# A hybrid decoder layer: k's normed blocks in the convolution's buffers, k's products in the common banks, v's first products bank by bank, and the square root behind the exponentials

## The chip, the cores and the metric

The program runs on one core of a Trainium2 chip. The metric is the device time of one execution in microseconds (us). Five engines work side by side, each through its own queue in the order written there: TensorE (PE, matrix products), VectorE (DVE), ScalarE (ACT), GpSimd (POOL) and SyncE (SP, which only issues transfers). An instruction that waits holds back everything behind it on its engine.

## The reference, cut to what matters

```python
x = x + 0.5 * swiglu(rms_norm(x, g1), ...)          # first feed-forward
h = rms_norm(x, gm)
xr, gate, q, k, v = split(h @ w_in)                 # 512 columns each
xc = causal_conv4(xr) + conv_b                      # RG-LRU branch
r, i = sigmoid(blockdiag(w_a) xc + b_a), sigmoid(blockdiag(w_x) xc + b_x)
a = exp(8 * r * log_sigmoid(lam));  b = sqrt(1 - a * a) * (i * xc)
h_t = a_t * h_(t-1) + b_t                           # a scan over 512 positions
y_rnn = h * gelu(gate)
q, k = rms_norm per head of 64;  z = q @ k.T        # stick-breaking attention
w = exp(log_sigmoid(z) + sum of log_sigmoid(-z) over the later keys);  y_att = w @ v
x = x + concat(rms_norm(y_rnn), rms_norm(y_att)) @ w_out
x = x + 0.5 * swiglu(rms_norm(x, g2), ...)          # second feed-forward
```

All data is float32; the sequence has 512 positions and the model 1024 columns.

## The kernel before, in words

Every large product is three matrix products of rounded parts (`mm3`, lines 137 to 139): weights and activations are split into a high part `h_`/`xh_` (a copy on ACT, line 127) and a low part `l_`/`xl_` (a subtraction on DVE, line 129). Weights come in by SP through three raw buffers `r_` and four buffers each of `h_` and `l_`.

The layer has a first feed-forward (`a`), the mixer, and a second feed-forward (`b`). The change lies in the mixer's projections, about 435 to 500 us into the span. There TensorE runs the column blocks one after another: four pairs of recurrence input and gate (`pxr`, `pga`, j = 0 to 3), then q after the second pair, k after the last, then v. Each of q, k and v is a set of four accumulators, one per 128 positions (`pk0` to `pk3`, `pv0` to `pv3`), filled over four weight tiles (`h_v0` to `h_v3`), each of two rows of 128 model columns. So a weight tile stands for 24 matrix products. Accumulators live in eight banks of PSUM, six under the tag `b` and two under the tag `y`, which are handed out in turn.

`gate(j)` computes the two block-diagonal products `pa`, `px` of the convolved block (in `xch`/`xcl`) in the two `y` banks. ACT makes of them `dec` (sigmoid), `tau` (tanh) and `ix` (sigmoid), and POOL multiplies `ix` by the convolved block. After the last, `gate(3)`, `recur` runs: exponentials of `dec`, one square root over all of `tau` (2048 columns), and on DVE, for each j, `ix` times `tau`, a second multiplication with `dec`, and the scan into `tau`. POOL multiplies the scan into `gel`. `rnn_out` splits `gel` into `yrh` (ACT) and `yrl` (DVE), and its squares are added up on POOL in `sqa_r`.

`norm_heads` norms k per head: ACT squares the accumulator (`nsqk`), DVE sums per head (`m8k`), POOL takes the power -0.5 (`r8k`), and DVE writes the normed block (`natk`) from the accumulator, which sets that bank free. `turn` transposes `natk` on TensorE into `ptk` (in a `y` bank); ACT and DVE write the split result `kTh`, `kTl`. When v's products are done, the sum of squares `pst_r`, the first output projection `po` and the attention's scores `pz` follow.

The order on each engine is not the order of the source: a scheduler orders the instructions at build time by its own estimate of times, and `issue_after` ties an instruction behind another. SP's order is the same in both kernels.

Of the kernel before, what the change touches and what calls it, by code (L numbers as in the profile page):

```python
# [8 lines left out]
F32 = mybir.dt.float32  # L9
F32R = mybir.dt.float32r  # L10
BF16 = mybir.dt.bfloat16
AF = mybir.ActivationFunctionType
# [3 lines left out]
P = 128  # L16
T = 512
D = 1024
KD = D // P
DFF = 2816  # L20
NF = DFF // P
DR = 512
NJ = DR // P
NB = T // P
# [25 lines left out]
def hybrid_layer_kernel(  # L50
# [17 lines left out]
    nc = tc.nc  # L68
# [21 lines left out]
    def bank(name, tag="b"):  # L90
        return banks["pool"].tile([P, T], F32, tag=tag, name=name, bufs=banks["tags"][tag])
# [40 lines left out]
    def weights_early(*args):  # L132
        with tc.high_priority(offset=200):
            return weights(*args)

    def mm3(out_, wh, wl, ah, al, start, stop):
        nc.tensor.matmul(out_, wh, ah, start=start, stop=False)  # L137
        nc.tensor.matmul(out_, wh, al, start=False, stop=False)  # L138
        nc.tensor.matmul(out_, wl, ah, start=False, stop=stop)  # L139
# [338 lines left out]
    neg_c = mp.tile([P, NJ], F32, tag="neg_c", name="neg_c", bufs=1)  # L478
# [19 lines left out]
    rp = rnn.enter_context(tc.tile_pool(name="rnn", bufs=1, reuse_waits="tile"))  # L498
    tau = rp.tile([P, NJ, T], F32, tag="tau", name="tau")
    dec = rp.tile([P, NJ, T], F32, tag="dec", name="dec")  # L500
# [66 lines left out]
    def recur():  # L567

        with tc.issue_after(box["gate"].ins):
            for j in range(NJ):  # L570
                nc.scalar.activation(dec[:, j, :], dec[:, j, :], AF.Exp, scale=neg_c[:, j : j + 1])
        last = nc.scalar.activation(tau, tau, AF.Sqrt)
        with tc.issue_after(last.ins):
            nc.scalar.activation(warm, mhalf, AF.Sigmoid)
        for j in range(NJ):
            nc.vector.tensor_mul(ix[j], ix[j], tau[:, j, :])
            nc.vector.scalar_tensor_tensor(
                ix[j], dec[:, j, :], 1.0, ix[j], op0=ALU.add, op1=ALU.mult
            )
            nc.vector.tensor_tensor_scan(  # L580
                tau[:, j, :], dec[:, j, :], ix[j], 0.0, op0=ALU.mult, op1=ALU.add
            )
            nc.gpsimd.tensor_mul(gel[j], gel[j], tau[:, j, :])
# [18 lines left out]
    v = []  # L602

    def project_qkv(c, n, between):
        pts = [bank(f"p{n}{b}", "y" if n == "k" and b < 2 else "b") for b in range(NB)]
        done = 0
        for kk in range(KD // 2):
            wh, wl = weights_early(w_qkv[c, kk], f"{n}{kk}")
            ks = (2 * kk, 2 * kk + 1)
            order = [(k, b) for k in ks for b in range(NB)]  # L610
            if kk == KD // 2 - 1:
                order = [(k, b) for b in range(NB) for k in ks]
            for k, b in order:
                t = slice(b * P, (b + 1) * P)
                s = slice((k % 2) * DR, (k % 2 + 1) * DR)
                mm3(pts[b], nm.h[k][:, t], nm.l[k][:, t], wh[:, s], wl[:, s], k == 0, k == KD - 1)
                done += 1
                if done in between:
                    between[done]()
        return pts  # L620

    def heads(ap):
        return ap.rearrange("p (h d) -> p h d", h=NH)

    def norm_heads(n, pts):
        nats = []
        for b in range(NB):
            rb = nm.r[:, b : b + 1]
            sq = rp.tile([P, DR], F32, tag="nsq", name=f"nsq{n}{b}", bufs=1)
            nc.scalar.activation(sq, pts[b], AF.Square, scale=rb)  # L630
            m = stat.tile([P, NH], F32, tag="m8", name=f"m8{n}{b}")
            nc.vector.tensor_reduce(m, heads(sq), axis=mybir.AxisListType.X, op=ALU.add)
            nc.vector.tensor_scalar(m, m, 1.0 / HD, EPS, op0=ALU.mult, op1=ALU.add)
            r = stat.tile([P, NH], F32, tag="r8", name=f"r8{n}{b}")
            nc.gpsimd.tensor_tensor(r, m, mhalf, op=ALU.pow)
            nat = rp.tile([P, DR], F32, tag="nat", name=f"nat{n}{b}", bufs=3)
            nc.vector.scalar_tensor_tensor(
                heads(nat),
                heads(pts[b]),
                rb,  # L640
                r.unsqueeze(2).to_broadcast([P, NH, HD]),
                op0=ALU.mult,
                op1=ALU.mult,
            )
            nats.append(nat)
        return nats
# [21 lines left out]
    convolve(0, *pj[0])  # L668
    convolve(1, *pj[1])
    pq = project_qkv(0, "q", {16: lambda: gate(0), 28: lambda: gate(1)})  # L670
    nq = norm_heads("q", pq)
    pj.append(project(2))
    convolve(2, *pj[2])
# [4 lines left out]
    def gate_and_recur():  # L678
        gate(3)
        recur()  # L680

    pk = project_qkv(1, "k", {8: gate_and_recur})
    nk = norm_heads("k", pk)
    pv = project_qkv(2, "v", {12: rnn_out, 27: lambda: turn("k", nk)})
    for b in range(NB):
        rb = nm.r[:, b : b + 1]
# [267 lines left out]
```

## Time and profile before

| what | value |
|---|---|
| median of 3 runs | 952.56 us (951.93 to 954.64) |
| the profiled execution | 952.85 us |
| its span, first to last instruction | 951.1 us |
| mean granted TensorE clock | 0.991 |
| busy PE | 928.4 us, 98% of the span |
| busy DVE | 675.0 us, 71% |
| busy ACT | 375.2 us, 39% |
| busy POOL | 111.1 us, 12% |

TensorE is busy nearly throughout, so a change can shorten the run only where TensorE stands idle or runs at a lower clock. In the rows, a time of one instruction is from its start to its end; matrix products overlap, so the pace of a row of them is read from the distance of their starts.

### The profile page before, as it was taken

What the parts mean: (1) busy time and instruction counts of PE and PEld (TensorE: products, weight loads), DVE (VectorE), ACT (ScalarE), POOL (GpSimd) and SP (SyncE); (2) the same over time, 40 slices, a digit from 0 to 9 for tenths busy, and PEclk for the clock granted to TensorE, in tenths of its full rate; (3) what the DMA queues carried; (4) which work ended last, traced back from release to release, by engine and by line L of the source; (5) the groups of instructions that cost most, each with busy time, mean ns of one, the idle gap of its engine ahead of it and who ended that gap; (6) DMA issues with size and microseconds to landing.
All of it is one profiled execution on the core that took longest, in us unless ns stands there. A gap on an engine that the chain in (4) does not pass through costs nothing.

```text
span 951.1 us, 12503 instructions
## 1 busy us (share of the span) xinstructions
PE 928.4 (98%) x4906; PEld 787.1 (83%) x4906; DVE 675.0 (71%) x1001; ACT 375.2 (39%) x529; POOL 111.1 (12%) x79
## 2 busy tenths in 40 slices
PE   8999999999999999999958999999999999999998
PEld 6888988898889888888845667888998899889987
DVE  7687867786768559673588867477776777677753
ACT  7233333333334334452647743343343333333430
POOL 4000000000000005543351121500000000000000
PEclk9999999999999999999979999999999999999999
DMA  7530443044302423322111112421152125212312
GB/s 244 178 110 1 151 138 111 1 135 154 110 2 72 150 75 116 120 84 83 34 34 34 45 67 89 159 100 52 67 178 89 66 68 177 89 67 67 105 52 89
DMA packets 27066, 89.44 MB, mean 94 GB/s; under 512 B 3072, under 2 KB 5376, under 8 KB 27008
## 3 DMA queue, kind: packets, MB, share of 16 engines
q1 hardware_dynamic: 27008, 88.65, 27.4%
q8 instruction: 39, 0.64, 0.3%
q14 instruction: 19, 0.16, 0.1%
HBM read 86.54 MB, written 2.10 MB: 93 GB/s over the span
## 4 chain that ended last, share of the span: by engine, by line
PE 87%; DVE 6%; DMA 3%; issue 1%; ACT 1%; SPq 1%; POOL 0%; DVEq 0%; ACTq 0%
PE pda L343 9%; PE pdb L343 8%; PE pga L137 5%; PE pga L139 5%; PE pga L138 5%; PE pub L137 4%; PE pub L139 4%; PE pgb L137 4%; PE pub L138 4%; PE pgb L139 4%; PE pgb L138 4%; PE pua L137 4%; PE pua L139 4%; PE pua L138 4%; PE po L137 1%
## 5 line engine op out<-in xcount | busy, mean ns | idle before, releaser
L343 PE MATMUL pdb<-bhb,l_db 128*128 128x256 f32 x252 | 70.6, 284 | 0.7 <-DVE l_db L129 0.7
L343 PE MATMUL pda<-bha,h_da 128*128 128x256 f32 x252 | 71.2, 284 | 0.0
L343 PE MATMUL pdb<-bhb,h_db 128*128 128x256 f32 x252 | 71.2, 284 | 0.0
L343 PE MATMUL pda<-bla,h_da 128*128 128x256 f32 x252 | 71.0, 283 | 0.0
L343 PE MATMUL pdb<-blb,h_db 128*128 128x256 f32 x252 | 71.0, 283 | 0.0
L343 PE MATMUL pda<-bha,l_da 128*128 128x256 f32 x252 | 70.5, 284 | 0.2 <-DVE l_da L129 0.2
L137 PE MATMUL pub<-xh_b,h_ub 128*128 128x512 f32 x176 | 68.7, 390 | 0.5 <-DVE yo L702 0.5
L137 PE MATMUL pgb<-xh_b,h_gb 128*128 128x512 f32 x176 | 68.6, 390 | 0.0
L139 PE MATMUL pgb<-xh_b,l_gb 128*128 128x512 f32 x176 | 68.5, 389 | 0.0
L138 PE MATMUL pgb<-xl_b,h_gb 128*128 128x512 f32 x176 | 68.5, 389 | 0.0
L138 PE MATMUL pub<-xl_b,h_ub 128*128 128x512 f32 x176 | 68.5, 389 | 0.0
L139 PE MATMUL pub<-xh_b,l_ub 128*128 128x512 f32 x176 | 68.5, 389 | 0.0
L137 PE MATMUL pga<-xh_a,h_ga 128*128 128x512 f32 x160 | 62.4, 390 | 0.0
L137 PE MATMUL pua<-xh_a,h_ua 128*128 128x512 f32 x160 | 62.3, 390 | 0.0
L139 PE MATMUL pga<-xh_a,l_ga 128*128 128x512 f32 x160 | 62.3, 389 | 0.0
L138 PE MATMUL pga<-xl_a,h_ga 128*128 128x512 f32 x160 | 62.3, 389 | 0.0
L139 PE MATMUL pua<-xh_a,l_ua 128*128 128x512 f32 x160 | 62.3, 389 | 0.0
L138 PE MATMUL pua<-xl_a,h_ua 128*128 128x512 f32 x160 | 62.2, 389 | 0.0
L167 POOL TENSOR_TENSOR sqa_m<-sqa_m,sq_m 128x512 f32<-128x512 f32 x7 | 11.8, 1680 | 325.9 <-issue 322.1
L343 PEld LDWEIGHTS pdb<-bhb,l_db 128*128 128x128 f32 x252 | 47.8, 192 | 1.2 <-DVE l_db L129 1.1
L246 DVE TENSOR_TENSOR uub<-pub,rb_b 128x512 f32<-128x512 f32 x22 | 15.2, 690 | 47.4 <-PE pub L139 47.4
L343 PEld LDWEIGHTS pda<-bha,h_da 128*128 128x128 f32 x252 | 48.3, 192 | 0.5
(318 smaller groups left out, 2460.4 us busy)
## 6 DMA issues: line engine op xcount, KB each, us to landing
r_gb<-in_wg SPq DMA_DIRECT2D x22, 512.0 KB, 3.3
r_ub<-in_wu SPq DMA_DIRECT2D x22, 512.0 KB, 3.3
r_ga<-in_wg SPq DMA_DIRECT2D x20, 512.0 KB, 3.3
r_ua<-in_wu SPq DMA_DIRECT2D x20, 512.0 KB, 3.4
rda<-in_wd SPq DMA_DIRECT2D x12, 768.0 KB, 4.9
rdb<-in_wd SPq DMA_DIRECT2D x12, 768.0 KB, 4.9
x<-in_xT SPq DMA_DIRECT2D x8, 256.0 KB, 4.6
r_da<-in_wd SPq DMA_DIRECT2D x4, 512.0 KB, 3.5
```

What stands on the lines that cost most here:

```text
L137: nc.tensor.matmul(out_, wh, ah, start=start, stop=False)
L138: nc.tensor.matmul(out_, wh, al, start=False, stop=False)
L139: nc.tensor.matmul(out_, wl, ah, start=False, stop=stop)
L167: nc.gpsimd.tensor_add(self.acc, self.acc, sq)
L246: nc.vector.tensor_mul(u, pu, rb)
L343: nc.tensor.matmul(pt, p[:, s], a, start=start and i == 0 and q == 0, stop=i == m - 1 and q == 2, skip_group_check=True,)
```

## The change

Four edits, all in the mixer:

- k's accumulators take four banks of the common tag `b`; before, the first two took the `y` banks that `gate(3)` needs next.
- k's normed blocks get buffers of their own, the convolution's `xch` and `xcl` (two each); before, they shared three buffers `nat` with q's.
- For v the first weight tile is used accumulator by accumulator (six products on `pv0`, then six on `pv1`, and so on), as the last already was.
- The square root is tied behind the exponentials.

```diff
         with tc.issue_after(box["gate"].ins):
             for j in range(NJ):
-                nc.scalar.activation(dec[:, j, :], dec[:, j, :], AF.Exp, scale=neg_c[:, j : j + 1])
-        last = nc.scalar.activation(tau, tau, AF.Sqrt)
+                last = nc.scalar.activation(dec[:, j, :], dec[:, j, :], AF.Exp, scale=neg_c[:, j : j + 1])
+        with tc.issue_after(last.ins):
+            last = nc.scalar.activation(tau, tau, AF.Sqrt)
...
     def project_qkv(c, n, between):
-        pts = [bank(f"p{n}{b}", "y" if n == "k" and b < 2 else "b") for b in range(NB)]
+        pts = [bank(f"p{n}{b}") for b in range(NB)]
...
-            if kk == KD // 2 - 1:
+            if kk == KD // 2 - 1 or n == "v" and kk == 0:
                 order = [(k, b) for b in range(NB) for k in ks]
...
-            nat = rp.tile([P, DR], F32, tag="nat", name=f"nat{n}{b}", bufs=3)
+            tag, bufs = ("nat", 3) if n == "q" else (("xch", "xcl")[b % 2], 2)
+            nat = rp.tile([P, DR], F32, tag=tag, name=f"nat{n}{b}", bufs=bufs)
```

The rows below are instructions in the order in which an engine gets them: line, operation, output, inputs, shape. The last gate on TensorE before, where `pa3` stands within v's first weight tile:

```order
L137 MATMUL pv3_4032<-h_v0_4035,xh_m1_3075 128x512
L137 MATMUL pa3_3868<-xch3_3824,bdha_3393 128x512
L138 MATMUL pa3_3868<-xcl3_3826,bdha_3393 128x512
L139 MATMUL pa3_3868<-xch3_3824,bdla_3395 128x512
L138 MATMUL pv3_4032<-l_v0_4037,xh_m1_3075 128x512
```

The same on TensorE now, with `px3` behind it, between k's first and second weight tile:

```order
L139 MATMUL pk3_3837<-h_k0_3840,xl_m1_3077 128x512
L137 MATMUL pa3_3868<-xch3_3824,bdha_3393 128x512
L138 MATMUL pa3_3868<-xcl3_3826,bdha_3393 128x512
L139 MATMUL pa3_3868<-xch3_3824,bdla_3395 128x512
L137 MATMUL px3_3872<-xch3_3824,bdhx_3399 128x512
L138 MATMUL px3_3872<-xcl3_3826,bdhx_3399 128x512
L139 MATMUL px3_3872<-xch3_3824,bdlx_3401 128x512
L137 MATMUL pk0_3834<-h_k1_3905,xh_m2_3123 128x512
```

The last gate has moved ahead by 72 products of k and 22 of v. ACT behind it, before:

```order
L630 ACTIVATE nsqk3_4020<-pk3_3837,r_m_3320 128x512
L555 ACTIVATE dec_3246<-pa3_3868,vec_71 128x512
L127 CAST h_o0_0_4242<-r_o0_0_4240 128x512
L556 ACTIVATE tau_3245<-dec_3246,half_c_3236 128x512
L572 ACT_TABLE_LOAD
L572 ACTIVATE tau_3245<-tau_3245 128x2048
L574 ACT_TABLE_LOAD
L574 ACTIVATE warm_69<-mhalf_67 128x8
L558 ACTIVATE ix3_3878<-px3_3872,vec_71 128x512
L571 ACT_TABLE_LOAD
L571 ACTIVATE dec_3246<-dec_3246,neg_c_3238 128x512 x4
```

And ACT now, ahead of v's second weight tile and of all of k's squares:

```order
L555 ACTIVATE dec_3246<-pa3_3868,vec_71 128x512
L558 ACTIVATE ix3_3878<-px3_3872,vec_71 128x512
L571 ACT_TABLE_LOAD
L571 ACTIVATE dec_3246<-dec_3246,neg_c_3238 128x512 x3
L556 ACTIVATE tau_3245<-dec_3246,half_c_3236 128x512
L571 ACTIVATE dec_3246<-dec_3246,neg_c_3238 128x512
L573 ACT_TABLE_LOAD
L573 ACTIVATE tau_3245<-tau_3245 128x2048
L575 ACT_TABLE_LOAD
L575 ACTIVATE warm_69<-mhalf_67 128x8
L127 CAST h_v1_4065<-r_v1_4063 128x1024
L127 CAST h_v2_4122<-r_v2_4120 128x1024
```

The exponentials now come ahead of the root (the one on line 573), and the sigmoid's table is loaded last; before, the exponential's was, and one more load stands ahead of the attention's first sigmoid (line 748).

DVE at k's norms, before, where they precede the recurrence (`L576` to `L580`):

```order
L129 TENSOR_TENSOR l_v2_4124<-r_v2_4120,h_v2_4122 128x1024
L632 TENSOR_REDUCE m8k0_3995<-nsqk0_3993 128x8
L633 TENSOR_SCALAR m8k0_3995<-m8k0_3995 128x8
L632 TENSOR_REDUCE m8k1_4004<-nsqk1_4002 128x8
L633 TENSOR_SCALAR m8k1_4004<-m8k1_4004 128x8
L637 SCALAR_TENSOR_TENSOR natk0_4000<-pk0_3834,r_m_3320,r8k0_3998 128x512
```

DVE now, behind eight multiplications of the recurrence and `l_v1`:

```order
L581 SCALAR_TENSOR_TENSOR tau_3245<-dec_3246,ix0_3517 128x512
L581 SCALAR_TENSOR_TENSOR tau_3245<-dec_3246,ix1_3578 128x512
L129 TENSOR_TENSOR l_v2_4124<-r_v2_4120,h_v2_4122 128x1024
L581 SCALAR_TENSOR_TENSOR tau_3245<-dec_3246,ix2_3787 128x512
L581 SCALAR_TENSOR_TENSOR tau_3245<-dec_3246,ix3_3878 128x512
L633 TENSOR_REDUCE m8k0_3995<-nsqk0_3993 128x8
L634 TENSOR_SCALAR m8k0_3995<-m8k0_3995 128x8
L129 TENSOR_TENSOR l_v3_4154<-r_v3_4150,h_v3_4152 128x1024
L633 TENSOR_REDUCE m8k1_4004<-nsqk1_4002 128x8
L634 TENSOR_SCALAR m8k1_4004<-m8k1_4004 128x8
L639 SCALAR_TENSOR_TENSOR natk0_4000<-pk0_3834,r_m_3320,r8k0_3998 128x512
```

POOL now at the same place; before, the four powers `r8k` came first, then `ix3`, the four products and the three sums:

```order
L559 TENSOR_TENSOR ix3_3878<-ix3_3878,xc3_3819 128x512
L584 TENSOR_TENSOR gel0_3406<-gel0_3406,tau_3245 128x512
L584 TENSOR_TENSOR gel1_3426<-gel1_3426,tau_3245 128x512
L584 TENSOR_TENSOR gel2_3694<-gel2_3694,tau_3245 128x512
L584 TENSOR_TENSOR gel3_3817<-gel3_3817,tau_3245 128x512
L167 TENSOR_TENSOR sqa_r_4085<-sqa_r_4085,sq_r1_4091 128x512
L636 TENSOR_TENSOR r8k0_3998<-m8k0_3995,mhalf_67 128x8
L167 TENSOR_TENSOR sqa_r_4085<-sqa_r_4085,sq_r2_4098 128x512
L636 TENSOR_TENSOR r8k1_4007<-m8k1_4004,mhalf_67 128x8
```

So `natk0` now stands behind the recurrence, on DVE and, through `r8k0`, on POOL. It matters to v: on TensorE now, the third accumulator `pv2` takes the bank of `pk0`, and its first product waits for `natk0`. It stands behind 46 products on `pv0` and `pv1`, over all four weight tiles:

```order
L139 MATMUL pv1_4030<-h_v3_4152,xl_m6_3146 128x512
L137 MATMUL pv1_4030<-h_v3_4152,xh_m7_3192 128x512
L137 MATMUL pv2_4031<-h_v0_4035,xh_m0_3028 128x512
L138 MATMUL pv2_4031<-l_v0_4037,xh_m0_3028 128x512
L139 MATMUL pv2_4031<-h_v0_4035,xl_m0_3030 128x512
```

Behind it come 13 products on `pv2`, 12 on `pv3` (which waits for `natk1`), 11 on both, the first two transposes of k, 14 more products, and the last two transposes. Before, each weight tile was used on all four accumulators before the next; the last transposes of k were the last thing there too.

## The prediction

> **What bounds the kernel now.** I read the list of waits first, for TensorE is busy for 98% of the span. The columns: who waited for whom, us in total, times, longest.
>
> ```profile
> PE ptk L653 <- DVE kTl L659: 10.3, 1, 10.3
> PE pw L771 <- DVE be L763: 3.3, 3, 1.5
> ```
>
> One wait stands out: k's third transpose waited 10.3 us for DVE to empty the bank. Then the table of windows around it (length, busy PE, PEld, DVE, ACT, POOL with counts, granted clock, DMA):
>
> ```profile
> 457.85:482.10 24.25, 24.25 (x111) 19.79 (x109) 16.21 (x22) 15.91 (x21) 9.56 (x6) 1.00 0.10 32
> 482.10:492.40 10.30, 0.03 (x2) 0.03 (x1) 10.30 (x10) 6.52 (x12) 8.63 (x5) 0.64 0.08 25
> 492.40:500.00 7.60, 7.60 (x28) 6.50 (x28) 2.77 (x5) 1.49 (x3) 1.02 (x1) 0.59 0.11 37
> ```
>
> In the gap DVE is full, and for 7.6 us after it TensorE runs at a clock of 0.59. The timeline of TensorE gives both costs (start, length, [idle before]):
>
> ```profile
> 436.09 0.39 PE L137 MATMUL pk<-h_k,xh_m 128*128 128x512 f32 x1
> ...
> 457.85 0.39 PE L137 MATMUL pv<-h_v,xh_m 128*128 128x512 f32 x1
> ...
> 462.83 0.40 PE L137 MATMUL pa<-xch,bdha 128*128 128x512 f32 x1
> ...
> 477.67 1.04 PE L653 MATMUL ptk<-ident,natk 128*128 128x128 f32 x8
> 478.46 0.47 PE L137 MATMUL pv<-h_v,xh_m 128*128 128x512 f32 x1
> ...
> 492.40 1.94 PE L653 MATMUL ptk<-ident,natk 128*128 128x128 f32 x8 [10.27 <-DVE kTl L659]
> ...
> 500.01 0.50 PE L734 MATMUL pz<-kTh,qTh 64*128 64x512 f32 x2
> ...
> 510.39 0.47 PE L137 MATMUL po<-yrh,h_o 128*128 128x512 f32 x1
> ...
> 513.22 0.71 PE L771 MATMUL pw<-ident,be 128*128 128x128 f32 x5
> ...
> 574.01 1.05 PE L174 MATMUL pst_t<-ones,sqa_t 128*128 128x1 f32 x8 [1.13 <-POOL sqa_t L167]
> ```
>
> A product's pace is (457.85 - 436.09) / 96 = 0.227 us. From 492.40 to 500.01, 7.61 us pass for eight transposes, eight sums and twelve `po`. At full clock these take 478.46 - 477.67 = 0.79, 1.05 and 513.22 - 510.39 = 2.83, together 4.67, so the low clock cost 2.94.
>
> Why was DVE late? `pa3` ran at 462.83, and ACT and DVE follow it:
>
> ```profile
> 441.73 1.06 ACT L127 CAST h_v<-r_v 128x1024 fp32r<-128x1024 f32 x1 [0.24 <-PE pk L139]
> 463.74 0.69 ACT L555 ACTIVATE dec<-pa,vec 128x512 f32<-128x512 f32 x1 [4.05 <-PE pa L139]
> 464.83 0.72 ACT L556 ACTIVATE tau<-dec,half_c 128x512 f32<-128x512 f32 x1
> 465.57 1.28 ACT L572 ACT_TABLE_LOAD   x1
> 466.87 1.92 ACT L572 ACTIVATE tau<-tau 128x2048 f32<-128x2048 f32 x1
> 472.20 2.57 ACT L571 ACTIVATE dec<-dec,neg_c 128x512 f32<-128x512 f32 x4
> 468.82 1.90 DVE L576 TENSOR_TENSOR ix<-ix,tau 128x512 f32<-128x512 f32 x3 [3.16 <-ACT tau L572]
> 475.38 2.33 DVE L580 TENSOR_TENSOR_SCAN tau<-dec,ix 128x512 f32<-128x512 f32 x2
> 477.63 1.71 DVE L129 TENSOR_TENSOR l_o<-r_o,h_o 128x512 fp32r<-128x512 f32 x1
> 491.51 1.40 DVE L659 SCALAR_TENSOR_TENSOR kTl<-ptk,vec,kTh 128x512 fp32r<-128x512 f32 x2
> 476.68 3.81 POOL L583 TENSOR_TENSOR gel<-gel,tau 128x512 f32<-128x512 f32 x2 [4.44 <-DVE tau L580]
> ```
>
> The recurrence starts on DVE at 468.8 and `kTl` stands behind it, until 491.5.
>
> **The change part by part.** *k in the common banks.* It adds no instruction. `gate(3)` runs after k's 24th product, at 436.09 + 24 x 0.227 = 441.5 instead of 462.8; six products then take 1.4 out of k's stretch instead of v's, at no net cost. `px3` ends at 443.1. ACT, free from 442.8 after `h_v0`, does `dec` and `ix` (0.58 each to the next start), a table load (1.28), three exponentials (0.64 each), the tanh, the fourth, a load and the root (1.92): it ends at 451.8, 17 us before 468.8.
>
> *Root behind the exponentials.* It puts 2.57 + 1.28 ahead of the root, counted above. `h_v1` waits behind it until 454.2; TensorE needs it at 459.3 + 12 x 0.227 = 462.0, so that is hidden. One of four loads goes:
>
> ```profile
> 500.52 1.28 ACT L748 ACT_TABLE_LOAD   x1
> 501.82 0.60 ACT L748 ACTIVATE s<-pz 128x512 f32<-128x512 f32 x1
> 500.91 0.28 PE L743 MATMUL pz<-fut_b,ident_b 128*128 128x128 bf16 x2
> ```
>
> The scores are there at about 501.2, so the first sigmoid can start 0.65 earlier, not 1.28. The scan behind it on DVE sets the next waits of TensorE: I take 0.65 (bounds 0 and 1.28).
>
> *k's norms and v bank by bank.* Here is the new wait. `natk` no longer waits for a transpose, but `natk0` now frees `pv2`'s bank and stands behind the recurrence. TensorE reaches `pv2` after 46 products, at 459.3 + 46 x 0.227 = 469.7. When is `natk0` done? DVE from 451.8: four times 0.6, `ix0` again 0.6, `l_v1` 1.15, three times 0.62, first scan 1.15: 459.0. From there DVE and POOL share the work, and rows show that they block each other:
>
> ```profile
> 455.84 3.24 POOL L635 TENSOR_TENSOR r8k<-m8k,mhalf 128x8 f32<-128x8 f32 x2 [12.98 <-DVE m8k L633]
> 470.96 1.28 POOL L559 TENSOR_TENSOR ix<-ix,xc 128x512 f32<-128x512 f32 x1 [7.14 <-ACT ix L558]
> 464.96 0.69 DVE L129 TENSOR_TENSOR l_o<-r_o,h_o 128x512 fp32r<-128x512 f32 x1 [1.96 <-ACT h_o L127]
> 489.84 0.74 DVE L637 SCALAR_TENSOR_TENSOR natk<-pk,r_m,r8k 128x512 f32<-128x512 f32 x1
> ```
>
> `l_o` takes 0.69 alone and 1.71 beside POOL's `gel` (477.63 above), a POOL product 1.28 alone and 1.9 beside DVE. That fits taking turns: about 1.1 for POOL, then 0.6 for DVE. In turns: second scan to 460.1, `gel0` 461.2, `l_v2` 462.4, `gel1` 463.5, two scans 465.8, `gel2` 466.9, `l_v3` 468.0, `gel3` 469.2, the sum 470.4, the power `r8k0` (1.62) 472.1, `natk0` 472.8. TensorE meets `l_v3` at 467.7, where it is 0.4 late, and `natk0` 2.7 late. `natk1` follows two POOL steps later, at 475.7, and 13 products cover that. The last transposes wait for `kTl0`: `natk3` at 480.2, then four `yrl` and three `l_o` at 0.6, then 0.65, ends at 485.1; TensorE is there at 485.0, so I count 0.2 for both.
>
> `yrh` now waits for v's last use of the buffers of x (480 instead of 479), still ahead of `kTh`. SP's order is unchanged: `h_o0`, 14 us later, delays the fourth output weights' transfer to about 485; `kTh` of the last blocks stands behind it and is ready at 488 to 489, `pz` is due at 490.
>
> Bounds of the wait for `natk0`: without any blocking it is done at 468.6, a wait of 0; with every POOL product at 1.92 after all of DVE's work, at 476.8, a wait of 6.6. The turns are seen in the rows, so I take 2.7.
>
> *The clock.* A gap can halve it afterwards. The windows of 1 us:
>
> ```profile
> 509.00:510.00 1.00, 0.00 (x0) 0.00 (x0) 1.00 (x3) 1.00 (x4) 0.00 (x0) 1.00 0.00 0
> 510.00:511.00 1.00, 0.92 (x6) 0.84 (x7) 1.00 (x3) 0.89 (x3) 0.00 (x0) 1.00 0.00 0
> 540.00:541.00 1.00, 0.00 (x0) 0.00 (x0) 1.00 (x4) 0.91 (x3) 0.00 (x0) 1.00 0.00 0
> 543.00:544.00 1.00, 1.00 (x5) 0.81 (x4) 0.87 (x2) 0.95 (x4) 0.00 (x0) 0.52 0.06 16
> 546.00:547.00 1.00, 1.00 (x5) 0.82 (x4) 1.00 (x2) 0.66 (x2) 0.00 (x0) 0.77 0.00 0
> 485.00:486.00 1.00, 0.00 (x0) 0.00 (x0) 1.00 (x1) 1.00 (x3) 1.00 (x2) 0.51 0.00 0
> ```
>
> The gap before 510 left it at 1.00. The gap of much the same length around 540 was followed by 3.4 us at half clock (543.0 to 546.3), which costs 1.7; in the long gap it fell 2.9 us after the start. A gap of 2.7 is nearer to those that tripped it, so I count 1.7 less the 0.2 of the transposes that it covers: 1.5 (bounds 0 and 3.4, two such stretches). The Trainium skill, "TensorE: Matmul & The Clock Gate", section "What's actually happening", says that the clock falls after at least one idle window of about 3.4 us; by that rule a gap of 2.7 costs nothing. The half clock after a gap of under 2 us speaks against it here, and I give it as a rival.
>
> **The sum**, against the profiled execution's 952.85: gone are 10.27 + 2.94 + 0.65 = 13.86; new are 0.4 + 2.7 + 0.2 + 1.5 = 4.8. That gives 943.8. The median, 952.56, lies 0.3 below that execution, so I forecast 943.5.
>
> **The rivals.**
> - *The clock stays up.* For it, the gap before 510; against it, the one at 540. 943.5 - 1.5 = 942.0.
> - *TensorE hardly waits at `pv2`.* If POOL and DVE block each other less, `natk0` comes by 470: the 0.4, 2.7 and 1.5 go, 938.9. Against it stand the `gel` rows at 1.9.
> - *`natk0` comes later still*, at the upper bound: 3.9 more, 947.4. For it, the 1.9 of all four `gel`; against it, that part of each 1.9 is DVE's turn, already counted.
> - *Slower: the wait moves to `pv2` and grows.* TensorE cannot pass `pv2`, and k's banks now hang on the recurrence. From the root's end to `natk0` I count 21 us. The gain of 9 is lost when it takes 30, `natk0` at 482; two us more make 955. That needs each of some twenty steps to be half as long again; the rows show 1.9 for 1.28 only in some.
> - *The change does not do what it says*, the last gate still late: 952.6. The orders of TensorE and ACT speak against it.
>
> **How the numbers follow.** Forecast 0.47, clock up 0.2, no wait 0.12, later 0.16, slower 0.03, nothing 0.02. About 0.3% (3 us) is what a measurement of this kernel can tell from no change; the first four all lie beyond it. So faster 0.95, same 0.02, slower 0.03. The range reaches down between the no-wait case and the clock case and up to the upper bound: 939.5 to 947.
>
> **What would show it.** Right: `pa` at 441.5, the root ending near 451.8, no wait of `ptk` over 1 us, a wait of `pv` for `natk` of 2 to 4 us at 470, half clock for some 3 us behind it, `pz` near 491, no table load at the first sigmoid. Wrong: a wait of `pv` above 6 us, or `pz` after 495, or a new wait in the attention stage, whose order I took to shift as a whole.

## The result and the profile after

The changed kernel takes 942.44 us (median of 4 runs, 940.50 to 944.91), the kernel before beside it 953.15 (4 runs, 951.93 to 954.64): a ratio of 0.9888, 95% interval 0.9858 to 0.9919. The profiled execution took 943.62, its span is 941.8.

TensorE's list of waits after (us in total, times, longest):

```profile
PE pw L773 <- DVE be L765: 3.3, 3, 1.5
PE pv L137 <- DVE natk L639: 2.4, 1, 2.4
```

The 10.3 us of `ptk` are gone; in their place stands one wait of 2.4 us for `natk0`. The timeline of TensorE after:

```profile
441.53 0.40 PE L137 MATMUL pa<-xch,bdha 128*128 128x512 f32 x1
...
467.44 0.39 PE L137 MATMUL pv<-h_v,xh_m 128*128 128x512 f32 x1
467.93 0.50 PE L138 MATMUL pv<-l_v,xh_m 128*128 128x512 f32 x1
...
472.71 0.80 PE L137 MATMUL pv<-h_v,xh_m 128*128 128x512 f32 x1 [2.44 <-DVE natk L639]
482.52 1.03 PE L655 MATMUL ptk<-ident,natk 128*128 128x128 f32 x8
486.60 1.03 PE L655 MATMUL ptk<-ident,natk 128*128 128x128 f32 x8
...
491.21 0.50 PE L736 MATMUL pz<-kTh,qTh 64*128 64x512 f32 x2
...
565.57 1.05 PE L174 MATMUL pst_t<-ones,sqa_t 128*128 128x1 f32 x8 [1.13 <-POOL sqa_t L167]
```

`pa` runs 21.3 us earlier than before. No transpose waits, and the scores (`pz`) start at 491.21 instead of 500.01. The chain that leads to `natk0`, on ACT, POOL and DVE, and the first sigmoid:

```profile
449.88 1.92 ACT L573 ACTIVATE tau<-tau 128x2048 f32<-128x2048 f32 x1
492.38 0.60 ACT L750 ACTIVATE s<-pz 128x512 f32<-128x512 f32 x1 [0.67 <-PE pz L745]
...
459.15 4.29 POOL L584 TENSOR_TENSOR gel<-gel,tau 128x512 f32<-128x512 f32 x2 [13.84 <-DVE tau L581]
464.59 4.43 POOL L584 TENSOR_TENSOR gel<-gel,tau 128x512 f32<-128x512 f32 x2 [1.16 <-DVE tau L581]
470.23 1.65 POOL L636 TENSOR_TENSOR r8k<-m8k,mhalf 128x8 f32<-128x8 f32 x1
...
471.91 0.75 DVE L639 SCALAR_TENSOR_TENSOR natk<-pk,r_m,r8k 128x512 f32<-128x512 f32 x1 [2.86 <-POOL r8k L636]
```

The root ends at 451.80; `natk0` follows 20.9 us later, at 472.66. The sigmoid starts 1.17 us after `pz` (before, 500.01 to 501.82, 1.81), with no table load ahead of it. The granted clock, in windows of 1 us where it changes (the number after POOL's count):

```profile
472.00:473.00 1.00, 0.29 (x1) 0.29 (x2) 1.00 (x2) 0.00 (x0) 1.00 (x1) 0.75 0.00 0
475.00:476.00 1.00, 1.00 (x4) 0.79 (x3) 1.00 (x2) 0.00 (x0) 1.00 (x2) 0.55 0.00 0
499.00:500.00 1.00, 0.15 (x2) 0.00 (x0) 1.00 (x2) 0.68 (x2) 0.00 (x0) 0.90 0.00 0
506.00:507.00 1.00, 1.00 (x7) 0.77 (x5) 1.00 (x2) 0.62 (x1) 0.00 (x0) 0.69 0.00 0
```

A window with a mean of 0.75 is one in which the clock fell (or rose) half way through. So it was halved from 472.5 to 475.9 and from 499.8 to 506.6. Before, it was halved once in the attention, from 543.0 to 546.5.

Of the 9.2 us by which the span is shorter, 8.80 lie ahead of `pz`. From `pz` to the sums `pst_t` the kernel now takes 74.36 instead of 74.00, and from there to the end 376.3 instead of 377.1.

### The profile page after: what moved, and what is told of

The parts are those of the page before. It is cut to its first block, busy times and chain, and to the rows that moved or that the text cites. A ratio compares the mean times of both kernels' runs of the same rounds, so it can differ in the third digit from the quotient of the medians.

```text
span 941.8 us, 12498 instructions
## 1 busy us (share of the span) xinstructions
PE 927.3 (98%) x4906; PEld 785.5 (83%) x4906; DVE 670.6 (71%) x1001; ACT 374.1 (40%) x528; POOL 110.9 (12%) x79
## 4 chain that ended last, share of the span: by engine, by line
PE 90%; DVE 4%; issue 2%; DMA 1%; ACT 1%; POOL 1%; SPq 1%; DVEq 0%; ACTq 0%; POOLq 0%
PE pda L343 10%; PE pdb L343 9%; PE pga L137 5%; PE pga L138 5%; PE pga L139 5%; PE pub L137 4%; PE pub L138 4%; PE pub L139 4%; PE pgb L137 4%; PE pgb L139 4%; PE pgb L138 4%; PE pua L138 4%; PE pua L137 4%; PE pua L139 4%; PE po L137 1%
## 5 line engine op out<-in xcount | busy, mean ns | idle before, releaser
L343 PEld LDWEIGHTS pdb<-bhb,h_db 128*128 128x128 f32 x252 | 48.2, 191 | 0.5
```

What stands on the lines that cost most here:

```text
L343: nc.tensor.matmul(pt, p[:, s], a, start=start and i == 0 and q == 0, stop=i == m - 1 and q == 2, skip_group_check=True,)
```

## The experiments

The ratios are to the kernel before, measured beside each kernel, with 95% intervals; medians measured at different times are better compared by them. The first two columns of times are read from the timeline of TensorE in each profile: from the last gate's `pa` to the first `pz`, and from there to `pst_t`. The last two count, for the same two stretches of the timeline, the spells of 3.41 us at half clock in them.

| kernel | median us | ratio | pa to pz | pz to pst_t | half clock, pa to pz | half clock, pz to pst_t |
|---|---|---|---|---|---|---|
| before | 953.15 | 1 | 37.18 | 74.00 | 4 | 1 |
| after | 942.44 | 0.9888 (0.9858 to 0.9919) | 49.68 | 74.36 | 1 | 2 |
| e1 banks alone | 943.67 | 0.9889 (0.9866 to 0.9913) | 48.21 | 74.50 | 0 | 2 |
| e2 all but banks | 950.29 | 0.9960 (0.9946 to 0.9974) | 31.34 | 77.62 | 2 | 4 |
| e3 norms first | 939.93 | 0.9850 (0.9826 to 0.9874) | 45.02 | 74.41 | 0 | 2 |
| e4 root first | 940.99 | 0.9860 (0.9839 to 0.9881) | 46.82 | 73.12 | 0 | 1 |
| e5 after again | 944.06 | 0.9897 (0.9880 to 0.9913) | 49.75 | 74.64 | 1 | 2 |
| e6 pairs | 944.01 | 0.9888 (0.9870 to 0.9906) | 48.13 | 74.73 | 0 | 2 |
| e7 gap filled | 943.96 | 0.9904 (0.9879 to 0.9928) | 49.29 | 74.37 | 0 | 2 |
| e8 root alone | 950.12 | 0.9958 (0.9942 to 0.9975) | 34.10 | 73.88 | 3 | 3 |
| e9 norms again | 939.40 | 0.9846 (0.9826 to 0.9866) | 45.03 | 73.16 | 0 | 1 |
| e10 both first | 938.93 | 0.9838 (0.9819 to 0.9857) | 45.02 | 73.15 | 0 | 1 |
| e11 attention filled | 934.13 | 0.9785 (0.9766 to 0.9805) | 45.03 | 69.34 | 0 | 0 |

In before, e2 and e8 `pa` stands late, in v's stretch, so their first column is compared only among themselves.

**One edit alone, and the other three.** The kernel before with the banks alone (e1), and the changed kernel without them (e2, the same two lines the other way round):

```
-        pts = [bank(f"p{n}{b}", "y" if n == "k" and b < 2 else "b") for b in range(NB)]
+        pts = [bank(f"p{n}{b}") for b in range(NB)]
```

> The kernel before with one of the four edits: k's products in banks of the common tag. Theory A (the early gate of the last recurrence block carries the whole gain): pa at about 441.5, the root ending near 452 although nothing ties it, the wait of pv for natk at 2 to 3 us, no wait of ptk over 1 us, pz near 491; 942 to 944 us, the same as the changed kernel. Theory B (the four buffers for the normed blocks carry part, since with three the last normed block waits for a transpose): the last transposes come 2 us or more later, pz after 493, 945 us or more. Theory C (the order that ties the root is needed): the root runs ahead of the exponentials, a table load stands ahead of the first sigmoid, 943 to 945 us.

> The changed kernel with k's first two products back in the banks of their own tag, the other three edits kept. Theory A: the last gate again runs in v's stretch, pa near 463; the root, now behind the exponentials, ends near 472, and TensorE loses about 10 us somewhere between 478 and 500, as before; 951 to 956 us, no gain. Theory B (buffers, v's order or the root's place carry the gain): 943 to 947 us.

TensorE and ACT in e1:

```profile
443.04 0.40 PE L137 MATMUL pa<-xch,bdha 128*128 128x512 f32 x1
474.22 0.50 PE L137 MATMUL pv<-h_v,xh_m 128*128 128x512 f32 x1 [2.45 <-DVE natk L637]
491.25 0.50 PE L734 MATMUL pz<-kTh,qTh 64*128 64x512 f32 x2
...
446.76 1.95 ACT L571 ACTIVATE dec<-dec,neg_c 128x512 f32<-128x512 f32 x3
451.38 1.92 ACT L572 ACTIVATE tau<-tau 128x2048 f32<-128x2048 f32 x1
```

Theory A holds. `pa` and all that follows it come 1.5 us later in this execution, on an order of instructions that is the same up to there, but the banks alone give the whole gain. The planner (the scheduler that orders the instructions) puts the root behind the exponentials without being told, and the wait for `natk0` is the same. In e2, without the banks, the long wait is there, but smaller, and the kernel is 0.4% faster than before; I had expected no gain. Its waits, and DVE:

```profile
PE ptk L655 <- DVE kTl L661: 5.6, 1, 5.6
PE pz L736 <- DVE kTl L661: 1.6, 1, 1.6
```

```profile
487.12 1.38 DVE L661 SCALAR_TENSOR_TENSOR kTl<-ptk,vec,kTh 128x512 fp32r<-128x512 f32 x2
488.42 3.30 DVE L591 SCALAR_TENSOR_TENSOR yrl<-gel,vec,yrh 128x512 fp32r<-128x512 f32 x2
```

`kTl` now stands ahead of the `yrl`, and comes at 487.1, where it came at 491.5 behind all four of them and a `natk`. The last `yrl` ahead of it in the kernel before:

```profile
490.50 1.09 DVE L590 SCALAR_TENSOR_TENSOR yrl<-gel,vec,yrh 128x512 fp32r<-128x512 f32 x1
```

To see which edit does that, the kernel before with the root's place alone:

```
-                nc.scalar.activation(dec[:, j, :], dec[:, j, :], AF.Exp, scale=neg_c[:, j : j + 1])
-        last = nc.scalar.activation(tau, tau, AF.Sqrt)
+                last = nc.scalar.activation(dec[:, j, :], dec[:, j, :], AF.Exp, scale=neg_c[:, j : j + 1])
+        with tc.issue_after(last.ins):
+            last = nc.scalar.activation(tau, tau, AF.Sqrt)
```

> The kernel before with one of the four edits: the root behind the exponentials. By the run without the banks, k's low parts on DVE stand ahead of three low parts of the recurrence's output, where before they stood behind four; this order comes with the root's place. Theory R (it is the root's place that won the 4 us there): the wait of ptk for kTl falls from 10.3 to about 6, with up to 1.6 more in pz; 949.5 to 951.5 us. Rival (it is the four buffers for the normed blocks, one of which stood right ahead of kTl): 952 us or more.

Its idle times of TensorE, and DVE:

```profile
488.56 1.94 PE L654 MATMUL ptk<-ident,natk 128*128 128x128 f32 x8 [6.32 <-DVE kTl L660]
496.39 0.50 PE L138 MATMUL po<-yrl,h_o 128*128 128x512 f32 x1 [1.47 <-DVE yrl L591]
...
487.04 0.72 DVE L638 SCALAR_TENSOR_TENSOR natk<-pk,r_m,r8k 128x512 f32<-128x512 f32 x1
487.68 1.39 DVE L660 SCALAR_TENSOR_TENSOR kTl<-ptk,vec,kTh 128x512 fp32r<-128x512 f32 x2
```

950.12, the same as e2, although a `natk` still stands right ahead of `kTl`: it is the root's place, through the order that the planner then gives DVE. Alone it wins 0.4%, on top of the banks nothing: both edits shorten the same wait, and the banks take it away.

**What `natk0` waits for.** e3 ties each scan of the recurrence behind the head sums of the same block of k, and each product `gel` behind its power; nothing else is edited. e4 turns the order of root and exponentials round:

```
+            with tc.issue_after(box["sumsk"][j].ins):
+                nc.vector.tensor_tensor_scan(
...
+            with tc.issue_after(box["powsk"][j].ins):
+                nc.gpsimd.tensor_mul(gel[j], gel[j], tau[:, j, :])
```

```
+            last = nc.scalar.activation(tau, tau, AF.Sqrt)
+        with tc.issue_after(last.ins):
             for j in range(NJ):
                 last = nc.scalar.activation(dec[:, j, :], dec[:, j, :], AF.Exp, scale=neg_c[:, j : j + 1])
-        with tc.issue_after(last.ins):
-            last = nc.scalar.activation(tau, tau, AF.Sqrt)
```

> The changed kernel, with k's norms ahead of the recurrence: each block's scan on DVE stands behind the head sums of the same block of k, and each product of gel and tau on POOL behind the power of the same block. Theory A (pv2 waits because natk0 stands behind four scans and four POOL products): natk0 is done by 465, the wait of pv for natk goes (2.4 us), the half clock behind it too (1.6 us), pz near 487; 937.5 to 939.5 us. Rival (the wait only moves: the recurrence is now late for the transposes, the sums of squares or the output products): a new wait of 2 us or more between 475 and 491, pz at 490 or later, 941 us or more.

> The changed kernel with the exponentials tied behind the root instead of the root behind the exponentials; ACT loads as many tables as in the changed kernel, so only the order differs: the root ends about 3.6 us earlier, near 448, and the exponentials at about 452. TensorE's order differs too: pv2 comes ten products (2.3 us) earlier. Theory A (natk0 follows the root on one chain through DVE and POOL): natk0 is done near 468 to 469.5, TensorE is at pv2 near 467, a wait of 1 to 2.5 us; 940 to 942.5 us. Rival (the chain starts at the exponentials, the scans wait for them): natk0 stays near 472.5 and the wait grows to 5 us, 943 to 945 us.

DVE's `natk0` and TensorE's `pz` in e3:

```profile
464.23 0.73 DVE L646 SCALAR_TENSOR_TENSOR natk<-pk,r_m,r8k 128x512 f32<-128x512 f32 x1
...
488.02 0.50 PE L744 MATMUL pz<-kTh,qTh 64*128 64x512 f32 x2
```

ACT's root, DVE's `natk0` and TensorE's wait in e4:

```profile
445.82 1.92 ACT L570 ACTIVATE tau<-tau 128x2048 f32<-128x2048 f32 x1
...
467.92 0.74 DVE L639 SCALAR_TENSOR_TENSOR natk<-pk,r_m,r8k 128x512 f32<-128x512 f32 x1
...
468.81 0.47 PE L137 MATMUL pv<-h_v,xh_m 128*128 128x512 f32 x1 [1.25 <-DVE natk L639]
```

In e3 `natk0` is done at 464.96 and no product of v waits for it; the wait does not move elsewhere. From `pa` to `pz` it takes 45.02, 4.7 less than after, where 2.4 of wait and 1.6 of half clock were expected to go. Some 0.4 of the rest is `l_v3`: in e3 it is in time, and after has lost that much against e3 one product later. The median came out 0.4 us above the range; in the profiled execution `pa` itself lay 1.5 us later than after. In e4 the root ends at 447.74, 4.1 us earlier, and `natk0` at 468.66, 4.0 earlier. So `natk0` follows the root, as theory A says, and not the exponentials: these now end at 451.63, where after they ended by 448.6, the table load of 1.28 ahead of the root. Both kernels are faster than e1, which equals the changed one and was measured beside them: the slowest executions are 940.74 (e3) and 941.71 (e4), the fastest of e1 is 942.12.

**The clock: the same program again.** A cell, below, is one stretch of 3.413 us between two possible changes of the clock.

> The changed kernel once more, for a second profile of the same program. Theory G (the clock is set on a grid of 3.413 us that does not start with the program: a cell of the grid in which TensorE is busy less than about 0.57 of the time is followed by a cell at half clock): the falls and rises of the granted clock lie whole multiples of 3.41 us apart, but at another phase than in the first profile, so that other gaps are followed by half clock; the wait of pv for natk stays at 2.4 us; 940 to 945 us. Rival (the clock follows the gap before it: a gap of 2.4 us is enough, one of 1.4 us not always): the 3.4 us at half clock stand right behind the gap at 470 again.

Its windows of 1 us in which the clock changes, and its wait:

```profile
473.00:474.00 1.00, 1.00 (x4) 0.79 (x5) 0.68 (x2) 0.46 (x1) 1.00 (x2) 0.74 0.00 0
476.00:477.00 1.00, 1.00 (x4) 0.75 (x4) 0.53 (x2) 0.00 (x0) 1.00 (x2) 0.55 0.00 0
500.00:501.00 1.00, 0.04 (x1) 0.04 (x1) 1.00 (x3) 1.00 (x4) 0.00 (x0) 0.90 0.00 0
504.00:505.00 1.00, 1.00 (x5) 0.78 (x5) 1.00 (x2) 0.89 (x2) 0.00 (x0) 0.90 0.00 0
534.00:535.00 1.00, 0.98 (x10) 0.56 (x7) 1.00 (x4) 0.66 (x3) 0.00 (x0) 0.96 0.00 0
538.00:539.00 1.00, 1.00 (x6) 0.78 (x5) 0.97 (x2) 0.80 (x2) 0.00 (x0) 0.83 0.00 0
```

```profile
472.97 0.50 PE L137 MATMUL pv<-h_v,xh_m 128*128 128x512 f32 x1 [2.45 <-DVE natk L639]
```

The clock falls and rises at 473.48, 476.90, 500.80, 504.20, 534.92 and 538.34. From the first these lie 3.42, 27.32, 30.72, 61.44 and 64.86 us away: 1, 8, 9, 18 and 19 times 3.413. In the first profile of the same program, 472.50, 475.90, 499.80 and 506.62 give 1, 8 and 10 times. The rival also expected half clock behind the gap at 470, and in this run it is there again; what speaks against it is e1, where a gap of the same 2.45 us is followed by none. The cells of the grid around that gap, of after and then of e1 (length, busy PE, ..., clock):

```profile
469.08:472.49 3.41, 1.19 (x6) 0.64 (x4) 0.58 (x1) 0.75 (x2) 3.41 (x3) 1.00 0.19 66
472.49:475.90 3.41, 3.19 (x8) 2.51 (x9) 2.09 (x5) 1.27 (x2) 3.41 (x3) 0.50 0.00 0
```

```profile
469.42:472.83 3.41, 2.33 (x9) 1.61 (x9) 1.11 (x2) 1.32 (x2) 3.41 (x3) 1.00 0.25 77
472.83:476.24 3.41, 2.02 (x9) 1.67 (x10) 1.51 (x3) 1.27 (x2) 3.41 (x4) 1.00 0.00 0
476.24:479.65 3.41, 3.41 (x17) 2.79 (x16) 2.04 (x4) 1.67 (x3) 3.41 (x3) 1.00 0.00 0
```

In after 2.2 us of the gap lie in one cell, which is busy for 1.19 of 3.41 us (0.35), and the next cell is at half clock. In e1 a border of the grid falls into the gap; the two cells are busy for 0.68 and 0.59, and the clock stays up. The gap is the same, the phase of the grid is not. What one such cell costs is read off the table: 49.68 and 49.75 from `pa` to `pz` with it, 48.21 (e1) without, so 1.5 us. e6, without one too, takes 48.13, but its gap is shorter. The executions that were not profiled point the same way. One cell at half clock lowers the mean granted clock of the changed kernel by 0.5 x 3.41 / 941.8 = 0.0018. The profiled execution, with three, has a mean of 0.995; the other three of after have 0.998, 0.995 and 0.996. So I estimate one to three cells in executions of one program; which gaps they followed is not on record.

**Filling the gap at `pv2`.** e6 writes v's products pair by pair; e7 adds eleven products of no use between the pairs:

```
+            if pair == (0, 1) and FILLERS:
+                spare = bank("spare", "y")
+                for _ in range(FILLERS):
+                    last = nc.tensor.matmul(spare, nm.h[k][:, t], wh[:, s], start=True, stop=True)
```

> Control for the next run: the changed kernel with v's products written pair by pair (pv0 and pv1, then pv2 and pv3), which moves two of TensorE's products among v's own. Both theories: as the changed kernel, a wait of pv for natk of 2.2 to 2.7 us at 470, 940 to 945 us; from the last gate's pa to pz 48.1 to 48.3 us if no half clock follows the gap, 49.6 to 49.8 if one cell does.

> The same with eleven needless products of 0.227 us into a free bank between pv1's and pv2's (2.5 us of work in the gap, no other use). Theory G (idle time in a cell of the grid sets the clock): pv waits under 0.3 us for natk, no half clock between 465 and 490 whatever the phase, from pa to pz 48.1 to 48.5 us; 0 to 2 us faster than the control, by how often the control's gap is followed by half clock. Rival (the products are only added time, the clock falls for another reason): from pa to pz 49.6 us or more, the same as or slower than the control.

TensorE in e6, where the wait is 2.00 us and so a little under the expected 2.2, and then TensorE and DVE in e7:

```profile
471.41 0.50 PE L138 MATMUL pv<-h_v,xh_m 128*128 128x512 f32 x1 [2.00 <-DVE natk L661]
```

```profile
470.43 2.66 PE L642 MATMUL spare<-h_v,xh_m 128*128 128x512 f32 x11
472.92 0.39 PE L138 MATMUL pv<-h_v,xh_m 128*128 128x512 f32 x1
...
475.55 0.47 PE L138 MATMUL pv<-h_v,xh_m 128*128 128x512 f32 x1 [1.11 <-DVE natk L661]
...
471.77 0.75 DVE L661 SCALAR_TENSOR_TENSOR natk<-pk,r_m,r8k 128x512 f32<-128x512 f32 x1 [2.86 <-POOL r8k L658]
```

This told little. `pv2` waits no more and there is no half clock, but the control had none in its profile either, and in e7 `pv3` now waits 1.11 us for `natk1`. From `pa` to `pz` that is 49.29, above what theory G allowed, and the medians are the same. The run shows only that `natk1`, 2.9 us behind `natk0` by way of POOL, is the next thing late at this place.

**Both orders, and the attention's gaps filled.** e9 repeats e3 as a control. e10 adds e4's edit to it. e11 adds to e3 eleven products of no use in a free bank, in the two gaps of 1.4 to 1.5 us of the attention:

```
+FILLERS = {((3,), (2, 3)): 6, ((3,), (6, 7)): 5}
...
+            if (qbs, pair) in FILLERS:
+                spare = bank("spare" + str(pair[0]), "y")
+                for _ in range(FILLERS[qbs, pair]):
+                    with tc.issue_after(last.ins):
+                        last = nc.tensor.matmul(spare, yrh[0][:, :P], yrh[0], start=True, stop=True)
```

> The kernel with k's norms ahead of the recurrence once more, as control for the next two. As in its first profile: no wait of pv for natk, from pa to pz 45.0 us, from pz to the sums of the attention's norm (pst_t) 74.4 us with two cells of the grid at half clock, or 72.7 with one, by the phase; 938.5 to 941 us.

> The same with the exponentials behind the root as well. Theory A: the wait of pv for natk is gone already, and nothing on TensorE waits for the chain that the earlier root shortens; from pa to pz 44.8 to 45.2 us, the same time as the control within 1 us. Rival (the recurrence is still late for the transposes or the sums of squares): from pa to pz 44 us or less, 1 to 2 us faster.

> The control with eleven needless products in a free bank, six in the first and five in the second of the two gaps of 1.4 to 1.5 us in which the attention's transposes wait for DVE; the planner moves some transposes and products of the attention with it. Theory G (idle time in a cell of the grid sets the clock): no cell at half clock between 485 and 560 us, from pz to pst_t 70.8 to 71.6 us, 936 to 938 us. Rival (the clock falls there for another reason, or the moved work eats the gain): half clock as before, or from pz to pst_t 73 us or more; 939 to 942 us.

e9 repeats e3 from `pa` to `pz`. Its attention takes 73.16, not 72.7, with one cell at half clock; e3, the same program, had two and took 74.41. e10 comes out as its control e9: 45.02 from `pa` to `pz`, 938.93 against 939.40. Once `natk0` is early, an earlier root buys nothing. The mean granted clock of e11, and its timeline of TensorE at the first gap and at `pst_t`:

```profile
core 0: 930.5 us, clock 1.000
```

```profile
492.17 1.63 PE L760 MATMUL spare<-yrh 128*128 128x512 f32 x6
493.83 0.55 PE L787 MATMUL pw<-ident,be 128*128 128x128 f32 x3
...
553.76 0.95 PE L175 MATMUL pst_t<-ones,sqa_t 128*128 128x1 f32 x8
```

With work added, the kernel is 5.3 us faster than its control, and the clock does not fall once: the mean is 1.000 in all four executions of e11, and 0.996 to 0.998 in those of e9 and e10. That is what theory G said of the clock, and against the rival. The stage is shorter than G alone allows (69.34, not 70.8 or more): the planner moved transposes and products of the attention as well, and `pst_t` no longer waits its 1.13 us. How much of the 3.8 us between 73.16 and 69.34 is clock and how much is this order was not separated. By the table one cell costs 1.2 to 1.6 us, and e9 has one there, so I estimate 2.2 to 2.6 for the order. The two profiled executions also differ by 1.7 us ahead of `pa`, where TensorE's order is the same, so how much of the 5.3 is the edit's is less sure than that it gains. At 934.13 us e11 is the fastest kernel here, 2.15% below before; of those that add no work, e3 and e10 are.

## Why the prediction was right, point by point

Forecast 943.5, measured 942.44; the sum against one profiled execution was 943.8, the profiled one took 943.62. Ahead of `pz` the sum had 13.21 gone and 4.8 new, so 8.4, and 8.80 were measured; the rest of the agreement is in part luck, as the last point says.

- *Gone, 13.86.* The wait of `ptk` went whole, as did the half clock behind it. The 0.65 of the table load went too (1.81 to 1.17 at the first sigmoid).
- *The early gate.* `pa` at 441.5 and the root's end at 451.8 came as worked out. e1 shows that the banks, and so this early gate, are the gain.
- *The wait at `pv2`.* 2.44 for 2.7 predicted; `l_v3` was 0.26 late for 0.4; the last transposes waited for nothing, for 0.2. From the root to `natk0` I had counted 21.0 us by letting DVE and POOL take turns, and 20.9 were measured. The steps between came as counted too: the last `gel` ended at 469.0 for 469.2, the power at 471.9 for 472.1. e3 and e4 moved `natk0` by the two ends of this chain.
- *The root's place.* Costed as worth only the 0.65 of its table load beside the banks. As an edit it is worth nothing there: e1 has the same order without the tie, the same 1.17 us from `pz` to the first sigmoid, and a ratio of 0.9889 for 0.9888. Nor is it the better order beside the banks: e4, with the root first and as many table loads, has `natk0` 4.0 us earlier. Alone the tie is worth 3.6 us (e8), by a change in DVE's order that I had not looked for, and so e2's expectation failed.
- *The clock behind the new gap.* 1.5 for 1.5: the 13 products from 472.71 took 4.57 us instead of 2.95. But the step was right by its size only, which is luck. I had taken the gap's length as what decides, and the rival "the clock stays up" as another way that the kernel could be. What decides is the phase as well: e1 had the clock up behind the same gap, and e6 behind one of 2.00 us. In the changed kernel itself both profiles show half clock there. The Trainium skill, "TensorE: Matmul & The Clock Gate", section "What's actually happening", says that the window is 3413 ns long and free-running; I had left out the second half. By that the traces agree to 0.02 us. It also says that the clock falls after at least one idle window, and there the traces differ: a cell that was busy for 0.35 or for 0.56 was enough.
- *The step that failed: "attention stage, whose order I took to shift as a whole".* Its order did, but for 4 of TensorE's 384 products; its time did not. From `pz` to `pst_t` it should have lost the 0.65 of the table load, and it gained 0.36. Before, one cell at half clock lay in it, after, two. Between profiles of otherwise equal stages one cell more makes 74.4 to 74.7 out of 73.1 to 73.2, so 1.2 to 1.6 us, which is more than the 1.0 missing. e3 and e9, the same program, show it alone: 74.41 with two cells, 73.16 with one. With one cell, as before had, e4, e9 and e10 take 0.9 less than before's 74.00. The loss was made good by 0.8 us behind `pst_t`, in the second feed-forward part, which the change does not touch; more than half of it is a wait for `l_db`, 0.7 in all before and 0.2 in this execution. That is luck: in e5, the same program, the part behind `pst_t` takes 377.3, no less than before.

## What to carry to other kernels

When one engine waits for another, work out where the late chain starts, not where it ends: here the tag of two banks held back a gate by 21 us, and the three other edits added nothing to what its change won. An edit's worth alone and its worth beside the others can be far apart (3.6 us and none), so a list of gains must not be summed without looking at which wait each of them shortens. A planner's order should be read again after every edit, since a tie on one engine can reorder another.

## What the runs showed of the hardware

The granted clock changes on a grid of 3.413 us. In the ten profiles of before, after and e1 to e8, in the part between 430 and 590 us, every fall and rise lies a whole number of cells from the others of its execution; the longest distance there, in e8, is 92.16 us for 27 cells. The phase differs from execution to execution. A fall lasts whole cells and follows a cell in which TensorE had idled. In that part all 12 cells at full clock that were busy for 0.56 of their length or less were followed by half clock; of the 20 that were busy for 0.57 to 0.69, 13 were; of those above, none. What decides between 0.57 and 0.69 stays open, and six more such cells near 20 us all kept the clock. In e9 and e10 a cell from 493.5, busy for 1.94 and 1.93 us (0.57), kept it in e9 and lost it in e10, so the busy share alone does not decide. The cells among v's long products (0.59, 0.68, 0.68, 0.69) kept the clock, most of those in the attention lost it. Why some falls last two cells or more stays open too.

It follows that gaps too short to count by themselves cost 1.2 to 1.6 us more in some executions, and that covering them, even with work of no use, can be faster than leaving TensorE idle (e11, where the moved order has a part in it). A TensorE stage compared between two profiles should have its cells at half clock counted first.
